# The first unit of weights in a one-core decoder step: three query blocks in six half-used banks, or a group's values in five whole banks

## The chip, the core and the metric

The kernel runs on one core of one Trainium2 chip. The metric is the device time of one execution in microseconds, lower is better. The engines are named as the profile names them: PE is the tensor engine's matmuls, PEld its weight loads, DVE VectorE, ACT ScalarE, POOL GpSimd, SP the engine whose queue issues every DMA of this kernel.

## The reference, cut to what matters

One layer of a decoder for 512 prompt tokens and 64 sample tokens (8 sequences of 8), model width 1024, all in float32. Only the front of it matters here.

```python
mod = silu(c) @ w_ada + b_ada                  # six modulations: sh1, sc1, g1, sh2, sc2, g2
u = x * (1 + sc1) + sh1
proj = u @ w_in                                # 1024 -> 10752 columns
qa, ka, va, qh, fh, ih, ogh, gate_a, gate_b = split(proj)
for gi, (win, dil) in enumerate(((128, 1), (512, 4), (2048, 16))):   # three groups of four heads
    prompt: banded attention over the tokens themselves
    sample: attention over a cache of 128, 512 or 1024 rows and the 8 new tokens
attn = groups merged by their log-sum-exp
hg = gated linear recurrence (HGRN2), 8 heads, over qh, fh, ih
mix = (sigmoid(gate_a) * (attn @ w_branch_a) + sigmoid(gate_b) * (hg @ w_branch_b)) @ w_out
x1 = layer_norm(a * x + g1 * mix);  x2 = layer_norm(a * x1 + g2 * mlp(x1))
```

The outputs are the new tokens, the new caches (mostly the old rows moved by 8) and the recurrence's states.

## The kernel before, in words

**Exact products.** Float32 operands are split into two parts (`whi` + `wlo`, `uh` + `ul`), and a product is the sum of three matmuls: `uh` with `whi`, `ul` with `whi`, `uh` with `wlo`. ACT makes the high part of the weights from the raw tile (`whi<-wraw`), DVE the rest (`wlo<-wraw,whi`).

**Units and blocks.** The weights are a list of units in a fixed order. A unit is 1024 rows by 512 or 256 columns; its raw rows arrive in tiles `wraw` of 1 MB, of which three exist (`NRAW`). Its blocks are of two kinds. A channel-major block holds 128 columns of weights in the array and moves the tokens past them: two halves of 288 tokens, each 24 matmuls of 128x288 (8 k's, that is blocks of 128 input channels, by three terms) into a bank of PSUM, of which it fills 288 of 512 columns. `q_block` and `k_block` are of this kind; a query's evacuation scales it on ACT (`qT<-lin`). A token-major unit (`tok=True`, `v_tokens`, `hi_tokens`) holds 128 tokens in the array and moves 512 columns of weights. `run_tokens` does so in two passes over five tiles of tokens: the first four k's into a bank that ACT copies out (`vtm<-lin`), then the other four, which DVE adds (`vtm<-vtm,lin`). The fifth tile is the samples: the 64 samples' high and low parts stand in the array together (`xs`), so it needs two matmuls for each k and a sum of the two halves of the rows (`vns`). The weights of a token-major unit are split by k (`split_k`), four k's just ahead of each pass.

**The start.** `ada` makes the first modulation in four steps s of two k's each, from eight loads `wada` a step. `make_u(k)` makes `uh` and `ul` of one k from x and the modulation: ACT and DVE for the prompt's 512 columns, POOL (`u`) for the samples' 64. Between these steps PE runs the unit that comes first, k by k, as far as its inputs are there (`early_mm`). Before the change that unit holds the queries of the last group (g = 2): three of its four blocks are computed so, in six banks (tags `lin`, `att` and `sx`, two each), and their first half of the weights is split before the modulation, the second half after step 1. The fourth query block and then the values of g = 2 follow in the ordinary loop. After the start POOL copies the samples' columns of `uh` and `ul` into `xs`, sixteen copies of 128x64 in one go.

**The order of the work.** The program is written out once, in Python, by a planner. `Engine` keeps a plan of when each instruction would end, and `Side` inserts pieces of other work between the matmuls of the main loop when the plan says their inputs are there: lane p is the prompt's attention and the recurrence's heads, r the recurrence's outputs and merges, n the new sample tokens, a the later modulations, s the samples' attention over the caches. Each engine then executes its instructions strictly in the order written. So where a piece stands on an engine is fixed by the plan, and how long it waits there by the chip.

**The samples' lane (s).** `sample_far(g)` for g = 2, then g = 1, then `sample_near` for g = 0. It is added when the last query block of its group is done. It turns the queries token-major (`qtm`), writes them to DRAM (`qsc`), reads them back spread over all partitions (`qb<-qsc`, `QB_AHEAD` of them ahead), multiplies each with cache rows on POOL (`qb<-qb,kv`, 32 products for g = 2, 64 for g = 1), adds up on DVE (`sc<-qb`), and after a softmax multiplies with the cached values on PE (`sx<-kv,pt`). `sample_merge` (`om`, `omg`, `ats`) ends the lane; with the prompt's merge (`og`, `Op`) it feeds the first branch's matmuls (`ath`, `atl`).

**The recurrence's heads.** Eight heads, each a chain through POOL (`hk`, `T`), DVE (`hq`) and PE; at a head's end stand POOL's `vm<-hvp,block_mask` and `S<-S,T`, DVE's chunk states `S<-S,T,att`, and PE's `att<-S,hq` and `att<-vm,ksm`.

Pages are tiles of 2.25 KB on each partition, `NPG` of them, for everything that passes through. All engine calls are recorded by one helper, so nearly every row of the profile says L173: rows are told apart by their tiles.

Of the kernel before, what the change touches and what calls it, by code (L numbers as in the profile page):

```python
# [51 lines left out]
NPG = 68  # L52
# [5 lines left out]
QB_AHEAD = 4  # L58
# [4 lines left out]
def shape_constants():  # L63
    """Masks, biases by position and the identity: they depend on the shapes alone."""
# [39 lines left out]
    # the even tokens' own keys come with the neighbours  # L104
# [4 lines left out]
class Engine:  # L109
    """An engine of the core whose instructions are also entered in a plan: when each would start and end by  # L110
    its size, by its place in the engine's queue and by the tiles that it reads and writes."""
# [7 lines left out]
    def enter(self, outs, ins, cost, latency=0.0, size=0):  # L119
        c = Engine  # L120
        at = c.clock[self.name]
        for t in ins + outs:
            end, by, lat = c.done.get(t.tensor.name, (0.0, None, 0.0))
            # transfers into one tile are apart from each other
            if not (size and by == "DMA" and t in outs):
                at = max(at, end if by == self.name else end + lat)
# [4 lines left out]
        if size:  # L131
            # one transfer that has to wait doesn't hold the others back
# [14 lines left out]
    def __getattr__(self, op):  # L147
        f = getattr(self.eng, op)

        def call(out, *args, **kw):  # L150
            aps = [a for a in list(args) + [v for k, v in kw.items() if k != "accum_out"] if isinstance(a, bass.AP)]
            outs = [out] + ([kw["accum_out"]] if "accum_out" in kw else [])
            if op == "dma_start":
                # the pieces of a result in DRAM are apart from each other
# [22 lines left out]
class Side:  # L177
    """Work that fills the tensor engine between the pieces of the linear layers: lanes of generators, each
    lane in order, the lanes of a class in turn. A generator yields what it has issued for the tensor engine
    (ns) and what its next piece has to wait for: a time, the tiles that it reads, or (None) everything that  # L180
    the piece has issued for the other engines. Each class of lanes gets its own share (rho) of the tensor
    engine's time."""
# [61 lines left out]
def decoder_step(ctx, tc, I, O):  # L244
# [13 lines left out]
    def store(dst, src):  # L258
        """A store is issued when its source is there, for the queue to hold up no load."""
        side.stores.append((dst, src))  # L260
# [10 lines left out]
    # ------------------------------------------------------------ constants  # L271
# [18 lines left out]
    # the first LayerNorm sees its input over ALPHA, and so its epsilon over the square  # L290
# [5 lines left out]
    # ------------------------------------------------------------ weights  # L296
# [23 lines left out]
    def load_more(force=False):  # L320
        """Loads into the slots that are free by now, or will be (force)."""
# [15 lines left out]
    def split(u, j):  # L337
        """The weights of one block of 128 columns as the exact sum of two parts."""
# [16 lines left out]
    def split_k(u, k, eng=V):  # L355
        """The same for 512 columns of one k."""
# [48 lines left out]
    def mm_tokens(w, xs, toks, ks, before=nothing, cols=slice(0, 512), tag="lin", n=128):  # L405
        """n tokens by 512 columns: the tokens stand in the array, the weights move."""
# [10 lines left out]
    def run_tokens(u, j):  # L417
        """Half of the k's for one tile of tokens; the second half adds to what the first has left."""
        blk = u["blocks"][j]
        c, ks = j % 5, range(j // 5 * 4, j // 5 * 4 + 4)  # L420
        if c == 4:
            # the samples' two parts stand in the array together
# [41 lines left out]
    # ------------------------------------------------------------ adaLN  # L464
# [3 lines left out]
    # sigmoid(x) = (tanh(x / 2) + 1) / 2: tanh stands in one table of the engine with exp  # L468
# [34 lines left out]
    def ada_load(s):  # L503
        """What the first modulation needs for two k's: 256 columns of its shift and 256 of its scale."""
# [6 lines left out]
    def ada(s, wk=None, u=None):  # L511
        """512 columns of the modulation: consecutive ones (u), or the first shift and scale of two k's (wk)."""
# [39 lines left out]
    # ------------------------------------------------------------ the order of the weights  # L552
# [9 lines left out]
    # ------------------------------------------------------------ attention state  # L562
# [25 lines left out]
    def toks(t, g, c):  # L588
        """The 128 prompt tokens of tile c: a natural block, or a residue mod 4; the tokens of the samples."""
        return t[:, NP:NT] if c == 4 else t[:, c * 128:(c + 1) * 128] if g == 0 else t[:, c:NP:4]  # L590
# [8 lines left out]
    def prompt_att(g, h):  # L599
# [5 lines left out]
        # token-major keys for the output  # L605
# [41 lines left out]
        # (query tile, key tile) pairs  # L647
# [36 lines left out]
    def merge_weights(st, n):  # L684
        """Weights of the three groups from their negated maxima and sums (st: [128, 3, 2, n])."""
# [77 lines left out]
    def kv_rows(g, x, r, ap, new):  # L763
        """The rows of tile r in a cache (or in the new cache, where the windows have moved on by 8 rows)."""
# [12 lines left out]
    def kv_more():  # L777
        """Cache rows ahead of their use: keys, then values, of one sequence after another."""
# [11 lines left out]
    def new_tokens(g):  # L790
        """The 64 new tokens: their rows of the new caches, and their part of the attention."""
# [46 lines left out]
    def pick(dst, src, first=None):  # L838
        """dst = the sum of the four parts of src, each by the mask of the partitions that it counts for."""
# [11 lines left out]
    def qb_more(g):  # L851
        """Queries on all partitions, ahead of their use: each key's own in the last group, or one for all keys."""
# [10 lines left out]
    def values(g, e, b, tiles, pms):  # L863
        """The sums over the keys of four tiles; the outputs come as 32 n + 8 h + t from tile n."""
# [11 lines left out]
    def sample_near():  # L876
        """The first group, four sequences' tiles of keys at a time, of which each counts for some of the
        queries. Partition 32 h + x is a head and a query's."""
# [35 lines left out]
    def sample_far(g):  # L914
        """The other groups, where few queries meet a key: their products with the keys are made and added up
# [1128 lines left out]
```

## Time and profile before

| | |
|---|---|
| timed runs (3) | 1388.92 us median, 1387.7 to 1394.49 |
| span of the profiled execution | 1384.2 us |
| its own time | not given; the timed runs lie 3.5 to 10.3 us above the span, their median 4.7 |
| PE busy | 1332.3 us (96%) |
| DVE / ACT / POOL busy | 774.9 / 468.6 / 360.4 us |
| DMA moved | 269.41 MB, mean 195 GB/s |

A row of a group reads: line, engine, operation, out<-in by the program's names, shapes, then how many, their busy time and the mean of one. A row of the timeline reads: start in us, duration in us, engine, operation, tiles, shape, and in brackets how long the engine stood idle before it and what ended that. The ends of matmuls are modelled; where their pace matters, the distance between their starts is used. A row of a table by stretches gives for each stretch its length and the busy time of each engine with the number of its instructions, and at the end the clock granted to PE as a share of full speed, the busy share of the DMA engines and GB/s.

### The profile page before, as it was taken

What the parts mean: (1) busy time and instruction counts of PE and PEld (TensorE: products, weight loads), DVE (VectorE), ACT (ScalarE), POOL (GpSimd) and SP (SyncE); (2) the same over time, 40 slices, a digit from 0 to 9 for tenths busy, and PEclk for the clock granted to TensorE, in tenths of its full rate; (3) what the DMA queues carried; (4) which work ended last, traced back from release to release, by engine and by line L of the source; (5) the groups of instructions that cost most, each with busy time, mean ns of one, the idle gap of its engine ahead of it and who ended that gap; (6) DMA issues with size and microseconds to landing.
All of it is one profiled execution on the core that took longest, in us unless ns stands there. A gap on an engine that the chain in (4) does not pass through costs nothing.

```text
span 1384.2 us, 24691 instructions
## 1 busy us (share of the span) xinstructions
PE 1332.3 (96%) x9624; PEld 1231.4 (89%) x9624; DVE 774.9 (56%) x1584; ACT 468.6 (34%) x1089; POOL 360.4 (26%) x419
## 2 busy tenths in 40 slices
PE   6999999999999899999999999999999999999995
PEld 3899899898878787888889999998999999999994
DVE  3456556558877886666655436547522333354458
ACT  3423222332332223332232442325554422423522
POOL 1232023016517573234343300002500200200205
PEclk9999999999999999999999999999999999999998
DMA  9799789689988887776454313331123533522322
GB/s 304 248 321 323 248 286 373 209 272 315 288 293 293 292 274 235 231 262 202 136 166 145 95 62 122 130 122 62 55 114 122 227 139 136 229 78 83 120 104 69
DMA packets 184521, 269.41 MB, mean 195 GB/s; under 512 B 15756, under 2 KB 92372, under 8 KB 183892
## 3 DMA queue, kind: packets, MB, share of 16 engines
q1 hardware_dynamic: 184404, 267.83, 57.4%
q8 instruction: 76, 1.25, 0.4%
q14 instruction: 41, 0.34, 0.1%
HBM read 210.45 MB, written 74.10 MB: 206 GB/s over the span
## 4 chain that ended last, share of the span: by engine, by line
PE 82%; DVE 6%; DMA 6%; ACT 2%; issue 1%; POOL 1%; SPq 1%; DVEq 0%; POOLq 0%; ACTq 0%
PE lin L173 67%; PE att L173 7%; PE tr L173 4%; PE sx L173 4%; DMA kv<-in_cache_kv_w_dram 2%; DVE wlo L173 2%; DMA out_dram<-kv 2%; DMA qb<-qsc 1%; DVE res L173 1%; SPq L173 1%; ACT whi L173 1%; DMA wraw<-in_w_ada_dram 0%; DMA xtm<-in_x_sample_dram 0%; DVE sc L173 0%; DVE st L173 0%
## 5 line engine op out<-in xcount | busy, mean ns | idle before, releaser
L173 DVE TENSOR_TENSOR wlo<-wraw,whi 128x512 fp32r<-128x512 f32 x340 | 252.4, 785 | 102.7 <-ACT whi L173 96.9
L173 PE MATMUL lin<-uh,whi 128*128 128x288 f32 x992 | 298.5, 301 | 4.3 <-DVE hso L173 2.4
L173 PE MATMUL lin<-ul,whi 128*128 128x288 f32 x992 | 299.3, 302 | 1.0 <-DVE ul L173 0.9
L173 PE MATMUL lin<-uh,wlo 128*128 128x288 f32 x992 | 298.0, 300 | 0.0
L173 ACT ACTIVATE whi<-wraw 128x512 fp32r<-128x512 f32 x344 | 193.1, 619 | 110.9 <-DMA wraw<-in_w_up_dram 42.0
L173 PEld LDWEIGHTS lin<-ul,whi 128*128 128x128 f32 x992 | 187.4, 189 | 13.6 <-issue 10.8
L173 PEld LDWEIGHTS lin<-uh,whi 128*128 128x128 f32 x992 | 187.6, 189 | 11.2 <-DVE hso L173 2.7
L173 PEld LDWEIGHTS lin<-uh,wlo 128*128 128x128 f32 x992 | 187.6, 189 | 3.7 <-issue 2.9
L173 POOL TENSOR_TENSOR qb<-qb,kv 128x512 f32<-128x512 f32 x96 | 129.7, 1369 | 208.5 <-DMA qb<-qsc 98.3
L173 PE MATMUL lin<-u2l,whi 128*128 128x288 f32 x496 | 146.8, 296 | 1.6 <-DVE u2l L173 1.6
L173 PE MATMUL lin<-u2h,whi 128*128 128x288 f32 x496 | 146.9, 296 | 1.3 <-ACT u2h L173 1.3
L173 PE MATMUL lin<-u2h,wlo 128*128 128x288 f32 x496 | 146.6, 296 | 0.0
L173 PE MATMUL lin<-hdh,whi 128*128 128x288 f32 (+1 forms) x448 | 133.7, 298 | 0.2 <-ACT hdh L173 0.2
L173 PE MATMUL lin<-hdl,whi 128*128 128x288 f32 (+1 forms) x448 | 133.1, 297 | 0.1
L173 PE MATMUL lin<-hdh,wlo 128*128 128x288 f32 (+1 forms) x448 | 133.1, 297 | 0.0
L173 POOL TENSOR_TENSOR rel<-rel 128x288 f32<-128x288 f32 x56 | 38.7, 690 | 292.8 <-ACT rel L173 287.8
L173 PEld LDWEIGHTS lin<-u2l,whi 128*128 128x128 f32 x496 | 93.1, 188 | 2.8 <-DVE u2l L173 2.3
L173 DVE TENSOR_TENSOR hdl<-rel,hdh 128x288 fp32r<-128x288 f32 x61 | 28.4, 465 | 118.8 <-ACT hdh L173 118.8
L173 PEld LDWEIGHTS lin<-u2h,whi 128*128 128x128 f32 x496 | 93.1, 188 | 1.8 <-ACT u2h L173 1.5
L173 PEld LDWEIGHTS lin<-u2h,wlo 128*128 128x128 f32 x496 | 93.1, 188 | 0.5 <-issue 0.5
L173 PEld LDWEIGHTS lin<-hdh,whi 128*128 128x128 f32 x448 | 84.1, 188 | 0.7 <-ACT hdh L173 0.4
L173 PEld LDWEIGHTS lin<-hdl,whi 128*128 128x128 f32 x448 | 84.1, 188 | 0.3 <-DVE hdl L173 0.3
(356 smaller groups left out, 2553.9 us busy)
## 6 DMA issues: line engine op xcount, KB each, us to landing
wraw<-in_w_in_dram SPq DMA_DIRECT2D x42, 1024.0 KB
kv<-in_cache_kv_w_dram SPq DMA_DIRECT2D x144, 256.0 KB
qb<-qsc SPq DMA_DIRECT2D x96, 256.0 KB
wraw<-in_w_down_dram SPq DMA_DIRECT2D x18, 1024.0 KB
out_dram<-kv SPq DMA_DIRECT2D x64, 256.0 KB
wraw<-in_w_ada_dram SPq DMA_DIRECT2D x16, 1024.0 KB
wraw<-in_w_up_dram SPq DMA_DIRECT2D x16, 1024.0 KB
out_dram<-in_cache_kv_w_dram SPq DMA_DIRECT2D x32, 512.0 KB
```

What stands on the lines that cost most here:

```text
L173: return f(out, *args, **kw)
```

## The change

The unit of the last group's values comes ahead of that group's queries, and so becomes the unit that is computed in the start. `early_mm` runs it token-major: for each k twelve matmuls of 128x512 into four banks (two of `lin`, two of `att`), and, one k later, two for the samples into one bank of `sx`. All eight k's add up in these five banks, so the unit is not passed over twice and nothing is added on DVE but the samples' two halves. The weights are split by k, four k's before the modulation and four after step 1, and the copies into `xs` stand at the end of each `make_u`. The four query blocks follow in the ordinary loop. Two numbers of the planner change with it: 70 pages instead of 68, and three spread queries ahead instead of four.

```diff
-NPG = 68
+NPG = 70
-QB_AHEAD = 4
+QB_AHEAD = 3
...
     for g in (2, 1, 0):
+        unit(w_in, 0, 8, 2 * QKV + g * 512, 512, [v_tokens(g)] * 10, tok=True)
         if g == 2:
             unit(w_in, 0, 8, g * 512, 512, [bind(q_block, g, h) for h in range(NH)])
-        unit(w_in, 0, 8, 2 * QKV + g * 512, 512, [v_tokens(g)] * 10, tok=True)
...
         V.tensor_sub(U_lo[k], t, U_hi[k])
+        for e, u in enumerate((U_hi[k], U_lo[k])):
+            G.tensor_copy(xs[k // 4][:, k % 4, e * NS:e * NS + NS], u[:, NP:NT])
...
-    n_early = 3
-    early = {}
-    def early_mm(k):
-        for j in range(n_early):
-            for h in range(2):
-                if k == 0:
-                    early[j, h] = bank([128, HF], ("lin", "att", "sx")[j])
-                mm_part(u0["w"][j], 8, u_x, h, early[j, h], (k,))
+    early_blk, n_early = u0["blocks"][0], len(u0["blocks"])
+    early = []
+    def early_mm(k, samples):
+        if not early:
+            early.extend(bank([128, 512], tag) for tag in ("lin", "lin", "att", "att", "sx"))
+        w = u0["w"][k]
+        if samples:
+            for m in range(2):
+                PE.matmul(early[4], xs[k // 4][:, k % 4], w[m], start=(k == 0 and m == 0), stop=(k == KT - 1 and m == 1))
+            u0["w"].pop(k)
+            return
+        for c in range(4):
+            for m, (xi, wi) in enumerate(TERMS):
+                PE.matmul(early[c], early_blk["toks"](u_x[xi][k], c), w[wi], start=(k == 0 and m == 0),
+                          stop=(k == KT - 1 and m == 2))
+        if k:
+            early_mm(k - 1, True)
...
-    for j in range(n_early):
-        done_split.add((id(u0), j))
-        split_slot(u0, j, 0)
+    done_split.update((id(u0), j) for j in range(n_early))
+    for k in range(4):
+        split_k(u0, k)
...
-            for j in range(n_early):
-                split_slot(u0, j, 1)
-    early_mm(KT - 1)
+            for k in range(4, KT):
+                split_k(u0, k)
+    early_mm(KT - 1, False)
+    early_mm(KT - 1, True)
...
-    for j in range(n_early):
-        for h in range(2):
-            u0["blocks"][j]["evac"](h, early[j, h])
-        u0["w"].pop(j)
+    def early_out():
+        for c, ps in enumerate(early):
+            t = early_blk["out"](c)
+            p = ps.rearrange("p (h d) -> p h d", d=128)
+            if c == 4:
+                A.activation(t, p[NS:128], AF.Copy)
+                V.tensor_add(t, t, p[0:NS])
+            elif c % 2:
+                A.activation(t, p, AF.Copy)
+            else:
+                V.tensor_copy(t, p)
...
-    for k in range(KT):
-        for e, t in enumerate((U_hi[k], U_lo[k])):
-            G.tensor_copy(xs[k // 4][:, k % 4, e * NS:e * NS + NS], t[:, NP:NT])
```

Since the planner places everything that comes later by its plan, the change also moves instructions far from the start. Three places are shown.

PE in the start, the last matmuls of one k of `early_mm` (k = 1 to 7). Before, the array holds the weights, and they end with the third query block, whose banks are `sx`:

```order
L173 MATMUL att<-uh,whi 128x288
L173 MATMUL att<-ul,whi 128x288
L173 MATMUL att<-uh,wlo 128x288
L173 MATMUL sx<-uh,whi 128x288
L173 MATMUL sx<-ul,whi 128x288
L173 MATMUL sx<-uh,wlo 128x288
```

After, the array holds the tokens, and two matmuls for the samples of the k before stand behind the four tiles:

```order
L173 MATMUL att<-whi,uh 128x512
L173 MATMUL att<-whi,ul 128x512
L173 MATMUL att<-wlo,uh 128x512
L173 MATMUL sx<-whi,xs 128x512
L173 MATMUL sx<-wlo,xs 128x512
```

For each k, eighteen matmuls of 288 columns have become fourteen of 512 (twelve for the first k).

ACT behind the start. Before, the fourth query block's evacuation is followed by the first pass of the values, and the splits of the weights for the second pass stand behind the fourth tile's evacuation (`whi` four times, one at once with the samples' tile between):

```order
L173 ACTIVATE qT<-lin 128x288 x2
L173 ACTIVATE vtm<-lin 128x512
L173 ACTIVATE qtm<-sx 64x512
L173 ACTIVATE vtm<-lin 128x512 x3
L173 ACTIVATE whi<-wraw 128x512 x4
L173 ACTIVATE vns<-lin 64x512
L173 ACTIVATE whi<-wraw 128x512 x6
```

After, the three evacuations of the start that are ACT's stand together, and a split of two instructions stands ahead of each query block:

```order
L173 ACTIVATE whi<-wraw 128x512 x2
L173 ACTIVATE vtm<-lin 128x512
L173 ACTIVATE vtm<-att 128x512
L173 ACTIVATE vns<-sx 64x512
L173 ACTIVATE whi<-wraw 128x512 x2
L173 ACTIVATE qT<-lin 128x288 x2
```

The values' second pass is gone, and `qtm`, with which the samples' lane begins, has moved behind all four query blocks.

POOL at the end of the recurrence's heads. Before, at the end of the first head, nine of the samples' products stand between `vm` and the states:

```order
L173 TENSOR_TENSOR qb<-qb,kv 128x512 x3
L173 TENSOR_TENSOR vm<-hvp,block_mask 96x512 x2
L173 TENSOR_TENSOR qb<-qb,kv 128x512 x9
L173 TENSOR_TENSOR S_4886<-S_4886,T 128x512
L173 TENSOR_TENSOR S_4887<-S_4887,T 128x512
L173 TENSOR_TENSOR qb<-qb,kv 128x512 x2
```

After, the first head's end has none, and the second head's end has this:

```order
L173 TENSOR_TENSOR qb<-qb,kv 128x512
L173 TENSOR_TENSOR vm<-hvp,block_mask 96x512 x2
L173 TENSOR_TENSOR qb<-qb,kv 128x512 x4
L173 TENSOR_TENSOR S_5278<-S_5278,T 128x512
L173 TENSOR_TENSOR qb<-qb,kv 128x512
L173 TENSOR_TENSOR S_5279<-S_5279,T 128x512
L173 TENSOR_TENSOR qb<-qb,kv 128x512 x2
```

The products of the samples' second group that stand among the heads are 32 in both. Before, 17 stand in the first head and 15 in the second; after, 11 in the second, 16 in the third and 5 in the fourth, and twelve more stand among and right behind the four pairs of multiplications of the prompt's merge (`og`), where before there was none.

More of the change, by code (lines that the diff above doesn't have):

```diff
@@ L1586, in decoder_step @@
         if s:
-            early_mm(2 * s - 1)
+            early_mm(2 * s - 1, False)
         if s == 2:
             next(shift[3])
-        early_mm(2 * s)
+        early_mm(2 * s, False)
         if s < 2:
@@ L1594, in decoder_step @@
         if s == 1:
-            for j in range(n_early):
-                split_slot(u0, j, 1)
-    early_mm(KT - 1)
+            for k in range(4, KT):
+                split_k(u0, k)
+    early_mm(KT - 1, False)
+    early_mm(KT - 1, True)
     shift.clear()
-    for j in range(n_early):
-        for h in range(2):
-            u0["blocks"][j]["evac"](h, early[j, h])
-        u0["w"].pop(j)
+    def early_out():
+        outs = []
+        for c, ps in enumerate(early):
[8 more added lines that the diff above has]
+                V.tensor_copy(t, p)
+            early_blk["done"](c, t)
+            outs.append(t)
+        early.clear()
+        early_blk["after"](outs)
+    early_out()
     kv_more()
-    for k in range(KT):
-        for e, t in enumerate((U_hi[k], U_lo[k])):
-            G.tensor_copy(xs[k // 4][:, k % 4, e * NS:e * NS + NS], t[:, NP:NT])
     for i, (u, j) in enumerate(flat):
```

## The prediction

> **What bounds the kernel.** I read the page first, then the busy time by stretches, PE's timeline over the first 95 us, and PE's waits from 320 us on.
>
> ```profile
> span 1384.2 us, 24691 instructions
> PE 1332.3 (96%) x9624; PEld 1231.4 (89%) x9624; DVE 774.9 (56%) x1584; ACT 468.6 (34%) x1089; POOL 360.4 (26%) x419
> ...
> 20.00:57.00 37.00, 32.06 (x230) 24.80 (x231) 16.71 (x35) 17.09 (x34) 12.23 (x32) 1.00 0.89 292
> 57.00:93.00 36.00, 34.81 (x167) 32.85 (x167) 14.26 (x21) 12.23 (x24) 8.47 (x6) 1.00 0.82 284
> 93.00:320.00 227.00, 226.77 (x1533) 209.22 (x1532) 134.50 (x265) 67.17 (x189) 49.40 (x39) 1.00 0.86 288
> 320.00:520.00 200.00, 183.98 (x1339) 163.04 (x1338) 157.00 (x291) 57.54 (x149) 109.39 (x98) 0.98 0.90 293
> ```
>
> PE is the bound, 96% of the span. So a change that leaves PE's matmuls as they are pays only where PE waits. The stretches say where that is: almost nothing from 93 to 320 us, 16 us from 320 to 520 us, where DVE (157 of 200 us) and POOL (109) are at their fullest, and a few microseconds in each of the first two. The change touches the first two directly and 320 to 520 us through the planner.
>
> **The matmuls themselves.**
>
> ```profile
> 34.56 0.30 PE L173 MATMUL lin<-uh,wlo 128*128 128x288 f32 x1
> 36.56 0.29 PE L173 MATMUL sx<-uh,wlo 128*128 128x288 f32 x1
> 66.91 0.40 PE L173 MATMUL lin<-whi,ul 128*128 128x512 f32 x1
> 75.13 0.39 PE L173 MATMUL lin<-whi,xs 128*128 128x512 f32 x1
> ```
>
> Between the first two rows lie fifteen starts, 0.133 us each; between the last two thirty-five, 0.235 us each. Three query blocks are 144 matmuls, 19.2 us; the values' unit is 112, 26.3 us. The start therefore has 7.1 us more to do, and the stretch behind it 7.1 us less, since three query blocks move there. That nets to nothing. Nor does the longer unit fill much idle time: of the 4.9 us that PE lacks from 20 to 57 us, most stands ahead of the unit's first matmul and at the transposes of x, where it can't go.
>
> **The waits that go.**
>
> ```profile
> 33.74 0.29 PE L173 MATMUL lin<-uh,whi 128*128 128x288 f32 x1
> 34.33 0.40 PE L173 MATMUL lin<-ul,whi 128*128 128x288 f32 x1 [0.30 <-DVE ul L173]
> 76.97 0.40 PE L173 MATMUL lin<-whi,uh 128*128 128x512 f32 x1
> 80.98 0.62 PE L173 MATMUL lin<-wlo,uh 128*128 128x512 f32 x1 [0.60 <-DVE wlo L173]
> 82.65 0.40 PE L173 MATMUL lin<-whi,ul 128*128 128x512 f32 x1
> 92.72 0.29 PE L173 MATMUL lin<-uh,whi 128*128 128x288 f32 x1
> 75.39 0.60 ACT L173 ACTIVATE vtm<-lin 128x512 f32<-128x512 f32 x1 [2.28 <-PE lin L173]
> 75.88 2.18 ACT L173 ACTIVATE whi<-wraw 128x512 fp32r<-128x512 f32 x4
> 58.00 2.50 DVE L173 TENSOR_TENSOR wlo<-wraw,whi 128x512 fp32r<-128x512 f32 x4 [0.32 <-ACT whi L173]
> 76.54 4.99 DVE L173 TENSOR_TENSOR wlo<-wraw,whi 128x512 fp32r<-128x512 f32 x4 [12.51 <-ACT whi L173]
> 73.20 7.18 POOL L173 TENSOR_TENSOR qb<-qb,kv 128x512 f32<-128x512 f32 x5 [16.49 <-DMA qb<-qsc]
> ```
>
> *The second pass of the values.* From 76.97 to 82.65 us thirteen matmuls start, 5.68 us where 3.05 would do: 2.63 us lost. The splits for this pass stand behind ACT's evacuation at 75.39, and DVE's four take 4.99 us instead of the 2.50 at 58.00, beside POOL's products. With the unit in the start, all eight splits are done long before their k's turn; behind it each query block needs two splits, which stand a block (48 x 0.133 = 6.4 us) ahead, and POOL has no products yet. I take 2.6 us, with 1.5 as the low end (one split late for the first query block, 0.6 for each of ACT and DVE).
>
> *The wait for `ul` at 34.33* (0.59 between starts where 0.133 would do, 0.46 lost) is covered by 0.9 us more PE work for each k (14 x 0.235 - 18 x 0.133). The splits after step 1 are four instead of three, 0.62 us more on DVE ahead of step 2's modulation; PE reaches that two k's (1.8 us) later than before, so it stays hidden. If that cover is thinner than I think, it costs its 0.6. Sum of the start: -3.1 us, from -1.4 to -4.
>
> *POOL's copies* now stand between one k's sums and the next's.
>
> ```profile
> 52.51 0.23 POOL L173 CAST xs<-ul 128x64 fp32r<-128x64 f32 x1
> 52.69 0.76 POOL L173 CAST xs<-uh 128x64 fp32r<-128x64 f32 x1
> 66.81 0.58 ACT L173 ACTIVATE qtm<-sx 64x512 f32<-64x512 f32 x1
> L173 ACT ACTIVATE ats<-tr x2: 392/404/417, 695.9 to 727.7; 128x128 f32<-128x128 f32 x2
> L173 ACT ACTIVATE ath<-attn x4: 672/674/677, 764.3 to 773.2; 128x576 fp32r<-128x576 f32 x4
> L173 PE MATMUL lin<-ath,whi x64: 288/295/370, 815.1 to 840.4; 128*128 128x288 f32 x64
> ```
>
> A copy takes 0.23 us, or 0.76 beside DVE. They delay the second `ul` of a step by about 1 us (two copies, and the wait for the first `ul`), which PE takes up a whole k (3.3 us) later: nothing. The Trainium skill speaks against this move: "SBUF — State Buffer", section "SBUF: two separate sides", has it that DVE with two SBUF inputs and a GpSimd operation that reads SBUF exclude each other for a whole instruction. The two `wlo` rows agree (4.99 against 2.50 us). By that rule alone, if each of the eight steps lost one 0.23 us copy on PE's path, the start's sum would be 1.8 us smaller.
>
> **What else moves.** The loads on SP are as many and as large; the values' rows come first, and the four cache loads now stand behind one more weight tile, which costs nothing, since their products begin later still. Evacuation: DVE loses four additions of values and gains two copies, all off PE's path. The stores of x and the masks' loads, which count blocks, come some 20 us later and nobody is near them. The samples' lane is the real displacement: `qtm` at 66.8 us now stands behind all four query blocks, where the first keys' matmul stood at 92.72, so at about 92.7 - 3.1 + 1 = 91, so the lane starts 24 us later, and with three spread queries ahead it runs slower. Its end (`ats`, 727.7) moves to some 755 to 770; `ath` follows, and PE wants that at 815.1: covered by 30 us.
>
> **The recurrence's heads.** What the later lane does to 320 to 520 us is the larger term, and the less certain.
>
> ```profile
> PE att L173 <- DVE S L173: 4.6, 2, 3.2
> PE att L173 <- ACT junk L173: 4.3, 1, 4.3
> ...
> PE tr L173 <- DVE Op L173: 1.4, 1, 1.4
> ...
> 444.98 12.55 POOL L173 TENSOR_TENSOR qb<-qb,kv 128x512 f32<-128x512 f32 x9
> 502.51 7.92 POOL L173 TENSOR_TENSOR qb<-qb,kv 128x512 f32<-128x512 f32 x6
> 458.04 0.49 PE L173 MATMUL att<-S,hq 128*128 128x128 f32 x2 [1.41 <-DVE S L173]
> 468.69 0.47 PE L173 MATMUL att<-vm,ksm 96*128 96x512 f32 x1 [4.32 <-ACT junk L173]
> 512.00 0.49 PE L173 MATMUL att<-S,hq 128*128 128x128 f32 x2 [3.18 <-DVE S L173]
> 468.00:472.00 4.00, 3.31 (x15) 3.29 (x16) 2.25 (x4) 1.22 (x7) 0.00 (x0) 0.65 0.89 295
> ```
>
> PE's worst waits of the stretch stand at the ends of the first two heads, where POOL has nine products in a row (and PE then waits 1.41 + 4.32 us) and six (3.18 us). The first is followed by a granted clock of 0.65 over 4 us, 1.4 us more. Together 10.3 us. By these two, each further product in the row costs (5.73 - 3.18) / 3 = 0.85 us, so a row of four costs 1.5. After, the first head's end has none; the second's and the third's have four: 3.0 us. An estimate from two points: -7.3 us, with 0 (the waits come from the heads' own work) and -10.3 as ends. Against it: the merge of the prompt has twelve products among its multiplications. One of its transposes waited 1.4 us without them; three more of four could, 0 to 4.2, I take half, 2.1. And the second half of the values' products and the sums behind them now fall on heads 3 to 5; one wait like 1.4 us, say +1. Net -4.2 us.
>
> **Sum.** 1384.2 - 3.1 - 4.2 = 1376.9 us of span; the timed median lies 4.7 us above the span (1388.92 - 1384.2), so 1381.6 us, 7.3 us or 0.53% less.
>
> **The rivals.** *Only the start pays*: heads and merge wait as much as before, elsewhere. Speaks for it that the same 32 products stand among the heads. 1388.9 - 3.1 = 1385.8 us. *The product rows are all of it*: three ends of heads without waits and a merge that hides its products, 1388.9 - 3.1 - 10.3 = 1375.5 us. *The change does not do what it says*: the fourth split and the copies put a wait into the start as long as the one that goes; nothing gained anywhere, 1388.9 us. *Slower*: the products now meet three heads and the merge. If each of heads 2, 3 and 4 ends as head 1 did (5.73 + 1.4 = 7.1 us), that is 21.3 instead of 10.3 us, and with the start 1388.9 + 11.0 - 3.1 = 1396.8 us. It decides once the waits from 320 to 700 us grow by over 3.1 us; against it, no row of products there is longer than four. The Trainium skill, "TensorE: Matmul & The Clock Gate", on the HAM clock gate, has the array fall to half clock after an idle window of about 3.4 us; the 0.65 behind the wait of 4.32 us agrees, and by it each new wait of that length costs its clock too.
>
> **How the numbers follow.** 0.5%, 7 us, is about what a measurement of this kernel tells from no change. Forecast: 0.42; it straddles that bound, 0.25 faster, 0.17 the same. Product rows are all of it: 0.17, faster. Only the start: 0.23, of which 0.03 faster. Nothing: 0.08. Slower: 0.10. So faster 0.45, same 0.45, slower 0.10. The range reaches from below the second rival to above the fourth without the slower one: 1371 to 1391.5 us.
>
> **What would show it.** In the changed profile: no wait of PE for `wlo` before the first keys; the first keys' matmul about 3 us ahead of 92.72; `qtm` near 91 us; the first head's end without a wait, those of the next two below 2 us; `ath` before 800 us. Wrong would be a PE wait of 3 us or more at a head's end or at `Op`, or the query blocks waiting for `whi`.

## The result, and the profile after

The changed kernel takes 1397.3 us (median of 9 runs, 1395.77 to 1401.79) against 1390.09 us for the kernel before in the same comparison (9 runs): a ratio of 1.0054, 95% interval 1.0038 to 1.007. It is slower by 7.2 us, half a percent, and the interval is clear of no change. The forecast was 1381.6 us.

The page's first lines after:

```profile
span 1397.7 us, 24645 instructions
PE 1337.6 (96%) x9624; PEld 1233.8 (88%) x9624; DVE 780.0 (56%) x1580; ACT 467.6 (33%) x1087; POOL 366.5 (26%) x419
```

This execution took 1399.52 us, 1.8 us above its own span, and the other runs lie as far above theirs. The spans of the timed runs of before go from 1385.1 to 1390.7 us (12 runs of the first comparison below). So its profile, with 1384.2 us, shows a quick execution: the two profiles lie 13.5 us apart, the medians 7.2. What the profiles are read for is where PE waits, not the sum.

The table by stretches (busy time of PE, PEld, DVE, ACT, POOL; then the granted clock), first before, then after:

```profile
320.00:420.00 100.00, 92.93 (x617) 81.43 (x617) 77.03 (x156) 32.26 (x78) 39.52 (x31) 0.98 0.93 296
420.00:520.00 100.00, 91.05 (x724) 81.60 (x722) 79.97 (x137) 25.27 (x71) 69.86 (x68) 0.98 0.87 290
520.00:700.00 180.00, 176.27 (x1341) 148.77 (x1334) 114.23 (x276) 58.16 (x154) 58.82 (x80) 1.00 0.66 212
700.00:830.00 130.00, 129.94 (x1024) 121.89 (x1023) 65.65 (x150) 47.45 (x113) 36.18 (x44) 1.00 0.36 113
25.00:30.00 5.00, 4.40 (x35) 2.45 (x34) 0.34 (x2) 1.08 (x2) 0.00 (x0) 1.00 1.09 316
```

```profile
57.00:93.00 36.00, 36.00 (x249) 35.60 (x249) 11.96 (x22) 11.86 (x26) 2.80 (x6) 1.00 0.25 89
320.00:420.00 100.00, 84.49 (x520) 73.22 (x519) 86.61 (x138) 29.31 (x71) 56.68 (x40) 0.95 0.84 262
420.00:520.00 100.00, 99.95 (x802) 89.01 (x801) 68.23 (x152) 28.06 (x77) 50.01 (x56) 1.00 0.80 270
520.00:700.00 180.00, 172.58 (x1304) 144.87 (x1303) 126.04 (x261) 58.08 (x150) 82.10 (x93) 1.00 0.76 249
700.00:830.00 130.00, 123.78 (x961) 114.02 (x960) 59.72 (x148) 40.18 (x101) 33.42 (x44) 0.99 0.40 119
25.00:30.00 5.00, 5.00 (x24) 2.49 (x23) 0.76 (x1) 0.26 (x1) 1.03 (x2) 0.66 1.09 321
```

From 57 to 93 us PE no longer waits, and from 420 to 520 us it gets back 8.9 us. But it loses 8.4 us from 320 to 420 (and clock: 0.95), 3.7 from 520 to 700 and 6.2 from 700 to 830.

The last row of each table is a difference of clock in the start: from 25 to 30 us it is 0.66 after and 1.00 before, which is 1.7 us over these five. That is no mark of the new order. In the 18 profiles of this study the clock there lies between 0.50 and 1.00, low ones in both orders, and the profile of before is one of only three with 1.00; this is part of what made it quick.

Three readings say what the losses and gains are.

*The start.* The first keys' transposes and the samples' queries after, then the transposes before:

```profile
98.00 0.63 PE L173 MATMUL tr<-ident,kT 128*128 128x128 f32 x4
92.89 0.59 ACT L173 ACTIVATE qtm<-sx 64x512 f32<-64x512 f32 x1 [1.09 <-PE sx L173]
```

```profile
100.14 0.63 PE L173 MATMUL tr<-ident,kT 128*128 128x128 f32 x4
```

The start gains 2.1 us here. Over all profiles of this study the mean start of these transposes is 98.5 us in eight of the new order and 101.0 in ten of the old: 2.5 us.

*The heads' ends and the prompt's merge* (after):

```profile
452.73 0.39 PE L173 MATMUL att<-S,hq 128*128 128x128 f32 x2
458.39 0.40 PE L173 MATMUL att<-vm,ksm 96*128 96x512 f32 x1
496.21 0.39 PE L173 MATMUL att<-S,hq 128*128 128x128 f32 x2
374.09 2.55 POOL L173 TENSOR_TENSOR og<-og,mw 128x512 f32<-128x512 f32 x2 [2.02 <-ACT hvtm L173]
376.61 3.37 POOL L173 TENSOR_TENSOR qb<-qb,kv 128x512 f32<-128x512 f32 x2
379.94 2.48 POOL L173 TENSOR_TENSOR og<-og,mw 128x512 f32<-128x512 f32 x2
380.58 0.69 PE L173 MATMUL tr<-ident,Op 128*128 128x128 f32 x2 [3.38 <-DVE Op L173]
380.00:384.00 4.00, 3.42 (x12) 2.90 (x13) 3.90 (x5) 0.60 (x1) 4.00 (x3) 0.58 0.90 338
388.40 5.52 DVE L173 TENSOR_TENSOR wlo<-wraw,whi 128x512 fp32r<-128x512 f32 x4 [0.84 <-ACT whi L173]
```

The waits of 1.41, 4.32 and 3.18 us at the ends of the first two heads are gone: these rows have no bracket. In their place products stand between the merge's multiplications; PE waits 3.38 us for `Op`, its clock falls to 0.58 over four microseconds, and four `wlo` take 5.52 us instead of the 2.50 at 58 us before, behind which PE waits for `wlo`, `hvs` and `hso` up to 417 us.

*The sample merge* (after), SP's queue, then ACT and PE:

```profile
743.83 0.46 SPq L173 DMA_DIRECT2D om<-snew  x1
744.41 0.57 SPq L173 DMA_DIRECT2D om<-ssam  x1
745.02 3.15 SPq L173 DMA_DIRECT2D om<-ssst  x4
748.23 5.17 SPq L173 DMA_DIRECT2D om<-ssam  x8
...
757.30 14.06 SPq L173 DMA_DIRECT2D wraw<-in_w_in_dram  x4
762.65 1.15 ACT L173 ACTIVATE whi<-wraw 128x512 fp32r<-128x512 f32 x2 [11.17 <-DMA wraw<-in_w_in_dram]
764.34 0.66 PE L173 MATMUL sx<-ident,moda 128*128 128x128 f32 x4 [3.88 <-ACT moda L173]
765.00:769.00 4.00, 4.00 (x33) 3.66 (x33) 3.45 (x18) 1.56 (x4) 0.78 (x2) 0.58 0.79 251
```

And SP's queue before:

```profile
698.06 0.46 SPq L173 DMA_DIRECT2D om<-snew  x1
...
710.83 0.56 SPq L173 DMA_DIRECT2D om<-ssst  x1
...
712.11 0.45 SPq L173 DMA_DIRECT2D wraw<-in_w_in_dram  x1
```

Some twenty small loads, about 0.6 us each, hold SP for 13.5 us, and the weights' load comes behind them. ACT stands 11.17 us at the split of those weights; behind it in ACT's order stands the copy `moda`, for which PE waits 3.88 us; the clock of 0.58 behind it is 1.7 us more. Before the change the same batch holds SP just as long, from 698.06 to 711.4 us, with weights behind it too, and PE does not wait (129.94 of 130 us busy). So the batch is no longer than it was; what differs is how soon the weights behind it are wanted.

### The profile page after: what moved, and what is told of

The parts are those of the page before. It is cut to its first block, busy times and chain, and to the rows that moved or that the text cites. A ratio compares the mean times of both kernels' runs of the same rounds, so it can differ in the third digit from the quotient of the medians.

```text
span 1397.7 us, 24645 instructions
## 1 busy us (share of the span) xinstructions
PE 1337.6 (96%) x9624; PEld 1233.8 (88%) x9624; DVE 780.0 (56%) x1580; ACT 467.6 (33%) x1087; POOL 366.5 (26%) x419
## 4 chain that ended last, share of the span: by engine, by line
PE 59%; DVE 8%; issue 2%; DMA 2%; ACT 2%; SPq 1%; POOL 1%; DVEq 0%; POOLq 0%; ACTq 0%
PE lin L173 50%; PE att L173 4%; PE sx L173 3%; DVE wlo L173 2%; PE tr L173 2%; DVE res L173 1%; SPq L173 1%; DMA qb<-qsc 1%; DVE sc L173 1%; DMA S<-in_state_hgrn_dram 1%; DVE hq L173 0%; DVE Op L173 0%; DMA wraw<-in_w_in_dram 0%; ACT whi L173 0%; DVE st L173 0%
## 5 line engine op out<-in xcount | busy, mean ns | idle before, releaser
L173 DVE TENSOR_TENSOR wlo<-wraw,whi 128x512 fp32r<-128x512 f32 x340 | 255.5, 795 | 102.1 <-ACT whi L173 94.8
L173 PE MATMUL lin<-uh,whi 128*128 128x288 f32 x1024 | 308.3, 301 | 4.4 <-DVE hso L173 3.4
L173 PE MATMUL lin<-uh,wlo 128*128 128x288 f32 x1024 | 309.5, 302 | 0.6 <-DVE wlo L173 0.5
L173 PE MATMUL lin<-ul,whi 128*128 128x288 f32 x1024 | 308.9, 302 | 0.0
L173 PEld LDWEIGHTS lin<-uh,whi 128*128 128x128 f32 x1024 | 194.4, 190 | 12.5 <-issue 4.4
L173 PEld LDWEIGHTS lin<-ul,whi 128*128 128x128 f32 x1024 | 194.1, 190 | 11.9 <-issue 10.7
L173 PEld LDWEIGHTS lin<-uh,wlo 128*128 128x128 f32 x1024 | 194.3, 190 | 8.0 <-issue 6.1
```

The lines of the kernel that those rows point to most:

```text
L173: return f(out, *args, **kw)
```

## The experiments

Theory 1: the samples' lane, now later, puts POOL's products and SP's loads where others need DVE and SP. Theory 2: three spread queries ahead instead of four. Theory 3: any new plan shifts the waits, whichever part of the change made it. Ratios are to the kernel before, with 95% intervals.

**The numbers alone: old order, 70 pages, three ahead**

```
-NPG = 68             +NPG = 70
-QB_AHEAD = 4         +QB_AHEAD = 3
```

> The old order of units with the two other numbers of the change: 70 pages and three spread queries ahead. The start is as before (no gain). The start of the samples' lane is as before, but it runs slower: 6 of the second group's products stand among the multiplications of the prompt's merge (before: none, after the change: 12), and 3 at the end of the first recurrence head (before: 11). Theory 1, what costs is where the products stand, above all those in the merge: half of after's 12, so about half of the loss, before + 4 us (range +1 to +7), with a wait of PE at the merge's transposes (Op) as in the changed kernel (3.5 us there). Theory 2, three queries ahead is the whole loss (7.2 us of median, and the 2.1 us that the start gained): before + 9 us. Theory 3, any new plan moves the waits by some us either way: anything from -3 to +9. If the order of units is all of it: before, within 1 us.

1405.36 us, 1.0112 (1.0089 to 1.0135): far more than any theory gave.

```profile
PE sx L173 <- ACT moda L173: 13.2, 2, 6.9
```

Two waits for `moda`, 13.2 us together, where the changed kernel has one of 3.88. The same kernel profiled a second time (labelled old_q3_om; its loads are not in threes):

> A second look at the old order with three queries ahead and 70 pages (1405.4 us over six runs), to see whether its two waits for moda (7.1 and 6.5 us in the first look) stand in each execution: both theories of the sample merge expect them again, each over 5 us, at about 715 and 763 us; waits that come and go with the loads would differ by more than 3 us.

1401.3 us in its one run; 12.6 us in two waits. They stand in both profiles.

**The new order with four ahead**

```
-QB_AHEAD = 3         +QB_AHEAD = 4
-if n_run == 6:       +if n_run == 2:     (x stored and given up)
```

> The new order of units with four spread queries ahead, as before the change. For the pages to suffice, the channel-major x is stored and given up after the second block instead of the sixth behind the start. The start is that of the changed kernel; the lane begins late but runs as fast as before: 5 products in the merge (after the change: 12), 5 at the first head, 15 at the second, 12 at the third. Theory 1 (where the products stand, above all in the merge): start -2.1 us, and 5/12 of about +9, so before + 2 us (range -1 to +5). Theory 2 (three queries ahead is the loss): before - 2 us. If the order of units is the loss whatever the queries: before + 7, as after the change. Theory 3 (any new plan): anything from -5 to +9.

1404.62 us, 1.0095 (1.0076 to 1.0115), with two waits for `moda` of 7.8 us together. Four queries ahead cure nothing, which theory 2 had as the whole loss.

**The old order with a late lane**

```
-NPG = 68             +NPG = 70
 q_block:   -if h == NH - 1:   +if h == NH - 1 and g < 2:
 v_tokens:  +if g == 2: side.add("s", sample_far(2))
```

> The old order of units and four queries ahead, and only the samples' lane is put off: it is added behind the values' unit instead of behind the last query block, so that it begins about 26 us later, as it does in the changed kernel (24 us there). 70 pages. No gain at the start. 9 products stand in the merge, none at the first head's end, 12 at the second, 14 at the third, 6 at the fourth. Theory 1 (the late lane is the loss): 9/12 of the changed kernel's +9 us behind the start, before + 7 us (range +4 to +10), with a PE wait of 2 us or more at Op and the waits at 420 to 520 us smaller than before's 9 us. Theory 2 (three queries ahead): before, within 1 us. Theory 3: anything from -3 to +9.

1405.94 us, 1.0117 (1.0099 to 1.0135); waits of 8.3 us for `moda` in two, 5.2 for `Op`. A late lane does it without the new order, but it costs 16 us where 4 to 10 were expected, and the next run shows that it isn't needed either.

**The old order, planner's allowance changed**

```
-LAT = 250.0          +LAT = 300.0
```

> The old order of units and the numbers of before, but the planner's allowance for a side step's inputs (LAT) is 300 ns instead of 250. Nothing is asked of the chip that before does not ask; only the order of the pieces shifts a little, and the samples' lane with it: 5 products stand in the merge, 8 at the first head, 16 at the second, 8 at the third. Theory 1 (products in the merge and at later heads): 5/12 of about +9, before + 4 us (range +1 to +6). Theory 2 (three queries ahead): before, within 1 us. Theory 3 (any new plan moves the waits by some us): a move of 2 us or more in either direction, for which no part of the change is needed.

1397.85 us, 1.0057 (1.0037 to 1.0078), 5.0 us for `moda` and 5.6 for `Op`. A change that asks nothing new of the chip costs as much as the one under study. Theories 1 and 3 are hard to tell apart here: each of the four new plans waits for `moda`, 5 to 13 us, and three of them for some 4 us or more at `Op`. So the next runs take away one meeting at a time. The thinned kernels and those with products on DVE keep every instruction in its place; the loads in threes and the held products make a new plan from that point on.

**The products, cut short in place**

```
-G.tensor_mul(p, p, kv[k])
+nc.gpsimd.tensor_mul(p[:, 0:8], p[:, 0:8], kv[k][:, 0:8])   (g == 1; entered in the plan at full size)
```

The samples' scores of the second group are then left incomplete.

> The changed kernel with every instruction in its place, but each of the second group's 64 products on POOL multiplies 8 of its 512 columns (the samples' second group is not computed in full), so that a product takes some 0.1 us instead of 0.8 to 1.2. Theory 1 (the loss is where these products stand): the waits at Op (3.5 us and its half clock of 1.7), wlo, hvs and hso at 380 to 420 us and hq at 529 and 579 shrink to what the old order has without its products; with the wait of 4 us behind the sample merge's loads left, after - 11 us, 1386 us, and within 3 us of the old order with thin products plus that wait. Theory 3 (any new plan moves the waits, products or not): after - 3 us or less, 1394 us or more, with the waits at 380 to 420 us still there.

> The kernel before with every instruction in its place and the second group's 64 products cut to 8 of 512 columns in the same way. If the rows of nine and six products make the waits at the ends of the first two heads (5.7 and 3.2 us, and 1.4 of clock, as the prediction had it): before - 9 us, 1381 us, and no wait over 1.5 us at 458, 469 and 512 us. If those waits are the heads' own work: before, within 2 us. Beside the changed kernel thinned alike: theory 1 has the two within 3 us of each other but for the wait behind the sample merge's loads (5.7 us with its clock); theory 3 has them as far apart as the two kernels are, 7 us.

1381.1 us for the new order, 1377.02 for the old: 0.9933 (0.9909 to 0.9957) and 0.99 (0.9879 to 0.9921). A product cut short took 0.20 us, not the 0.1 that was expected, against 1.29 us in full. The table by stretches, new and old, where 184.44 and 183.98 us were busy:

```profile
320.00:520.00 200.00, 194.94 (x1445) 173.77 (x1444) 142.76 (x314) 61.47 (x156) 60.87 (x111) 0.98 0.88 290
```

```profile
320.00:520.00 200.00, 194.81 (x1430) 172.78 (x1430) 144.72 (x313) 61.72 (x159) 51.64 (x101) 0.99 0.95 313
```

So the waits at the first two heads' ends before were the products', as the prediction read them, and PE gets back 10 us in either order. All 64 products cost 16.2 us after the change (1397.3 - 1381.1; the two medians are of different comparisons) and 14.0 before (1391.03 - 1377.02): 0.25 and 0.22 us each in the mean. The wait for `moda` stands in the thinned new order, 3.8 us, so it is not the products'. What is left between the two thinned kernels, 4.1 us, is near that wait with its clock (5.6) less the start's gain (2.5), 3.1.

**The sample merge's loads in threes**

```
 for i, (p0, col, src) in enumerate(sample_rows(g, e)):
     SP.dma_start(t[p0:p0 + n, col:col + src.shape[-1]], src)
+    if i % 3 == 2:
+        yield 0, 2000
```

> The changed kernel, but the sample merge issues its twenty loads on SP three at a time, with a pause of 2 us of the plan behind each three, so that loads of weights can go between them. All instructions up to about 700 us stand as in the changed kernel. If these loads ahead of the weights' are what PE waits for at 764 us (moda, 4.0 us, and its half clock of 1.7): after - 5.7 us, 1391.6 us (range 1390 to 1394), no wait for moda over 1 us. If the weights' loads were late for another reason (the slots in use until then): after, 1397 us, with the wait still there. The waits up to 700 us and their clocks are not touched in either case.

1390.51 us, 0.9999 (0.9984 to 1.0013): 6.8 us less than the changed kernel (again between two comparisons). SP now, and ACT's copy:

```profile
750.43 1.92 SPq L173 DMA_DIRECT2D om<-ssam  x3
753.28 1.23 SPq L173 DMA_DIRECT2D wraw<-in_w_in_dram  x2
754.56 2.38 SPq L173 DMA_DIRECT2D om<-ssam  x3
754.14 0.60 ACT L173 ACTIVATE moda<-sx 128x512 f32<-128x512 f32 x1 [4.37 <-PE sx L173]
```

The weights go between the small loads, and `moda` waits for PE, not for ACT. The same edit in the old order with three ahead:

> The old order with three queries ahead and 70 pages (1405.4 us), and the sample merge's loads in threes with pauses. If these loads ahead of the weights' are most of what that kernel lost: its two waits for moda (7.1 and 6.5 us) and their half clocks (1.7 each) go, 1405.4 - 15, some 1390 us (1388 to 1394), so the order of units is not needed for the loss nor for its cure. If the loads are not the cause: 1400 us or more.

1387.88 us, 0.9982 (0.9966 to 0.9999), 17.5 us less than without it. These loads were most of what that kernel lost; the new order is not needed for their collision.

**No products during the prompt's merge, by the plan and in place**

```
 sample_far:    +while merging[0]: yield 0, 500     (ahead of each product; set while prompt_merge's heads run; loads in threes too)
```

> As the one before, and the samples' lane issues no product while the prompt's merge runs, so that POOL has only the merge's multiplications there (in the changed kernel 12 products stand among them). The products move on to the first, second and third head. Theory 1 (products in the merge cost 3.5 us at Op and 1.7 of clock): 1391.6 - 5, some 1387 us, below the kernel before; the wait at Op 1.6 us as before the change. Theory 3 (any plan other than the one that before happens to have costs 7 to 16 us, as the first four runs show): 1395 us or more, with new waits of 2 us and more at other places.

1384.34 us, 0.996 (0.994 to 0.998): faster than both kernels. Theory 3 had 1395 us or more for it and failed here. With the order kept, and the products among the merge's multiplications cut short:

> The kernel with the sample merge's loads in threes (1390.5 us), every instruction in its place, and the eleven products that stand among the prompt merge's multiplications on POOL cut to 8 of 512 columns (those scores are not computed in full). It prices these eleven by themselves, with no new plan. If they make the wait at Op (3.8 us there) and the waits that follow at wlo, hvs, hvtm and hso up to 420 us (3.8 against 2.6 before the change at hso alone): 1390.5 - 6, some 1384.5 us, as the version gives that holds the products back (1384.3), with Op near 1.6 us. If that version's gain comes from the new plan behind the merge instead: within 2 us of 1390.5.

1383.22 us, 0.9945 (0.9927 to 0.9962): eleven products among the merge's multiplications cost 7.3 us, 0.66 each, against 0.25 for the mean product. The merge is a far dearer place for them than the mean.

**The old order with the same cures**

> The old order of units with all else as in the version that beat both kernels (three queries ahead, 70 pages, the sample merge's loads in threes, no products while the prompt's merge runs). It shows what the new order of units itself is worth once the two collisions are gone: if the start's gain, 2.0 us by the starts of the first keys in five profiles of each order, is all, 1384.3 + 2, some 1386 us (1384 to 1389); if a late lane still costs, the old order is faster, 1382 us or less; if plans scatter by chance, anything from 1380 to 1395.

1398.05 us, 1.0059 (1.0038 to 1.0081). That is outside every range given. DVE, POOL, ACT and PE at its worst wait:

```profile
524.42 7.40 DVE L173 TENSOR_TENSOR wlo<-wraw,whi 128x512 fp32r<-128x512 f32 x4
523.81 2.03 POOL L173 TENSOR_TENSOR vm<-hvp,block_mask 96x512 fp32r<-96x512 f32 x2 [0.23 <-DMA out_dram<-kv]
525.81 4.26 POOL L173 TENSOR_TENSOR qb<-qb,kv 128x512 f32<-128x512 f32 x3
532.16 0.54 ACT L173 ACTIVATE ksm<-tr 32x128 fp32r<-32x128 f32 x2 [6.97 <-DVE ksm L173]
534.00 1.11 PE L173 MATMUL sx<-ident,moda 128*128 128x128 f32 x4 [5.25 <-ACT moda L173]
```

Read upward: PE waits for `moda`, which stands on ACT behind `ksm`, which waits for DVE's half of it, which stands behind four `wlo`, which take 7.40 us beside POOL's rows. With the products cut in place:

> The old order with both cures (1398.05 us), every instruction in its place, the second group's 64 products on POOL cut to 8 of 512 columns (those scores are not computed in full). If the meeting of the products with DVE's wlo is what made that kernel 12 us slower than expected: 1398 - 18, some 1380 us, within 4 us of the other two thinned kernels (1377.0 and 1381.1), the wait for moda at 534 us and the one for wlo at 582 us gone. If its new plan is slow for other reasons: 1388 us or more, with those waits still there.

1380.92 us, 0.9916 (0.9899 to 0.9932): 17 us less, and within 4 us of the other thinned kernels. The wait for `moda` is gone. The four `wlo` there:

```profile
517.12 4.18 DVE L173 TENSOR_TENSOR wlo<-wraw,whi 128x512 fp32r<-128x512 f32 x4
```

They take 3.2 us less than the 7.40, but more than the 2.50 of other places: POOL's two `vm` still stand beside them, from 517.17 us on.

**The products on DVE, in place**

```
-G.tensor_mul(p, p, kv[k])
+nc.vector.tensor_mul(p, p, kv[k])       (entered in the plan as POOL's)
```

> The changed kernel with the sample merge's loads in threes (1390.5 us), and the eleven products that stand among the prompt merge's multiplications run on DVE instead of POOL, in the same places of the order; all is computed. DVE gets 11 x 0.65 = 7 us more in some 25 us, POOL 11 x 1.3 to 1.7 less. If the price of these products (7.3 us by the thinned run) is that POOL and DVE slow each other: 1385 us, half way to the thinned run or better. If it is their time in a queue that the merge stands in: 1390 us or more, as DVE is the fuller of the two there.

> As the one before, with all 64 products of the second group on DVE, in the same places of the order. DVE gets 64 x 0.65 = 42 us more between 250 and 600 us and loses what POOL took from it. If the meeting of the two engines is the price of all of them (13 to 16 us by the thinned kernels): some 1382 us. If DVE, busy for three quarters of that stretch already, becomes what PE waits for: 1395 us or more.

> The kernel before, with all 64 products of the second group on DVE instead of POOL, every other instruction in its place. Meeting of the two engines: before - 7, 1383 us, with the waits of 5.7 and 3.2 us at the ends of the first two heads halved or better (nine products in a row there are 5.9 us on DVE instead of 12.6 on POOL). DVE too full: before + 5 or more, with those waits longer.

1387.87 us (0.9979, 0.9964 to 0.9993) with the merge's products alone, 1383.03 (0.9932, 0.9917 to 0.9946) with all 64 and the loads in threes, 1384.87 (0.9946, 0.993 to 0.9961) for the kernel before with nothing else changed. The one with all 64 and the loads in threes:

```profile
320.00:520.00 200.00, 190.54 (x1385) 168.54 (x1383) 165.54 (x349) 60.45 (x155) 49.55 (x54) 0.97 0.86 277
378.78 0.69 DVE L944 TENSOR_TENSOR qb<-qb,kv 128x512 f32<-128x512 f32 x1
381.17 2.48 DVE L173 TENSOR_TENSOR wlo<-wraw,whi 128x512 fp32r<-128x512 f32 x4
```

DVE, the fuller engine, takes over all these products, and PE is busy 6 us more in this stretch than after the change (4.2 more than the 186.31 with the loads in threes alone): a product is 0.69 us there, and the four `wlo` are back at 2.48. The page of the kernel before with its products on DVE has

```profile
PE 1333.5 (97%) x9624; PEld 1231.6 (89%) x9624; DVE 787.3 (57%) x1648; ACT 469.0 (34%) x1089; POOL 278.4 (20%) x355
```

64 products at a median of 0.684 us are 43.8 us more for DVE, yet its busy time rises by only 12.4, from 774.9: all its other instructions together became 31 us shorter. In the old order 6.4 us of the products' 14.0 are gone and 7.9 are left (1384.87 - 1377.02); in the new order 7.5 are gone (1390.51 - 1383.03). So about half of the price goes when the products leave POOL, and DVE's shorter instructions speak for the meeting of the two engines as its cause. That the other half is the products' own time, in an order that DVE or POOL has to keep, was not tested by itself. Of the eleven in the merge, 2.6 of 7.3 us came back. The versions with all 64 on DVE and with the merge kept clear (1383.03, 1384.87 and 1384.34 us) beat both kernels by 6 us or more, and all three compute everything.

## Why the prediction was wrong

The account, in medians: +6.8 us for the sample merge's loads (changed kernel against loads in threes), +2.2 for the products (16.2 against 14.0), -2.5 for the start; together +6.5 of the 7.2 measured. The medians are of several comparisons, in which the kernel before stood between 1389.9 and 1391.3 us, so each term is uncertain by a microsecond or more. The forecast had 0, -4.2 and -3.1 in their place: the loads make 6.8 of the miss, the products 6.4, the start 0.6.

- *Start, -3.1.* Right in its mechanism (57 to 93 us is full, the copies cost nothing, since PE waits 0.4 us for `ul` where it waited 0.9, `qtm` at 92.89 where some 91 was said); the gain is 2.5.
- *Heads, -7.3.* Right on the spot: rows of products made those waits, and they went, 8.9 us by the table. Its price for the shorter rows that remain, 1.5 us each, was too high: PE shows no wait for `S` or `vm` at any head's end after the change.
- *Merge, +2.1, and heads 3 to 5, +1.* Mis-sized; with the next point these terms turned the sum. The eleven products cost 7.3 us at the merge, since not `Op` alone was late but also `wlo`, `hvs` and `hso`, which stand behind it on DVE, and PE's clock; from 520 to 700 us PE lost 3.7. The step that failed is to price a product's place by the one wait visible there. Cut short in place, the 64 turn out to cost nearly the same in either order (16.2 and 14.0 us), not 4.2 less.
- *"Covered by 30 us".* Wrong, and the largest single miss, 6.8 us. The lane's end was followed only to the one who wants its result: `ath` came at 791 us, in time. What else the moved step issues was not followed: the sample merge's loads passed into a part of SP's queue where weights are fetched that ACT splits ahead of `moda`. The sum had no term for that.
- *The slower rival* had the right size, 1396.8, and a chance of 0.10. Its mechanism holds by half: the waits from 320 to 700 us did grow by 3.2 us, at the merge and the later heads, but the head-ends it named did not repeat, and its 11 us did not come. The rest is SP's loads, which it did not have. That its number fits is luck.
- *The clock.* Both new waits of over 3 us cost their clock, as the rival's sentence had it: 0.58 over four microseconds at 380 and again at 765. The Trainium skill, "TensorE: Matmul & The Clock Gate", section "What's actually happening", has half clock after an idle window of about 3.4 us. The traces agree for long waits: between 40 and 1380 us the 18 profiles have 21 waits of PE of 3.3 us or more, and over the four microseconds behind each the clock is 0.50 to 0.67. Shorter waits go either way: the 3.18 us before the change cost nothing (1.00 from 512 to 516 us), and the same wait of 2.98 us for `qp` is followed by 1.00 in the changed kernel (333.9 to 337.9 us) and by 0.61 in the one with the merge kept clear (335.3 to 339.3 us).
- *The 4.7 us between median and span* were 1.8 of the run and 2.9 of a quick profiled execution. The forecast difference doesn't rest on them.

What stays open is the worth of the new order by itself. With the loads in threes and the same two numbers it stands at 0.9999 against 0.9982 for the old order, with the products on DVE at 0.9932 (loads in threes too) against 0.9946; the intervals overlap in both pairs. With the merge kept clear it is 0.996 against 1.0059, but there the old order's plan had met the products elsewhere (1380.92 us without them). Why a given plan meets the products at one head and not at the next was not tried.

## What to carry to other kernels

A step that moves takes along every queue it uses: follow its small loads to whoever loads behind them, not only its result to whoever reads it. Waits that come from two engines meeting move with the plan and don't go away; to price them, shorten one party with the order frozen, and to cure about half of them, as here, put the work on the engine that it collides with, if that has room. All four other plans that were tried first were slower, by 5.7 to 11.7 thousandths, one of them for a planner's constant alone. Whether the plan before is just a favourable one is not shown; but a change that also moves the plan should be compared with edits that only move the plan.

## What the runs showed of the hardware

One DVE instruction can last through several of POOL's. In the kernel before, all `wlo`, and the two that stand beside POOL's row of six products at the second head's end (502.51 us, 7.92 us long, shown in the prediction):

```profile
L173 DVE TENSOR_TENSOR wlo<-wraw,whi x340: 671/685/4572, 16.5 to 1366.0; 128x512 fp32r<-128x512 f32 x170
504.74 6.24 DVE L173 TENSOR_TENSOR wlo<-wraw,whi 128x512 fp32r<-128x512 f32 x2
```

The longest, 4.57 us against a median of 0.685, is the first of these two. It lasts as long as three and a half products of 1.32 us. The Trainium skill, "SBUF — State Buffer", section "SBUF: two separate sides", calls this an exclusive lock held for a whole instruction; the rows agree with that, and read so, DVE lost the lock several times running. And to move 43.8 us of work from POOL onto the fuller DVE made the kernel before 6.4 us faster.
